# A decoder block's first norm rearranged: four lo parts on GpSimd, c spread without a diagonal, squares in pairs, 1/rms on quarters of the tokens, two more load buffers

## The chip, the core and the metric

The kernel runs on one core of one Trainium2 chip. The metric is the device time of one execution in microseconds (us), as the median of several runs. The core has a matrix engine (TensorE, PE in the rows), VectorE (DVE), ScalarE (ACT), GpSimd (POOL), and a queue from which SyncE (SP) issues loads and stores. Each engine takes its own instructions strictly in the order of the program, and waits when an operand is not there yet.

## What is computed

One decoder block for 512 tokens of width 1024: a norm whose scale and shift come from a second input c, a projection, attention and a short convolution, an output projection, a second norm, and an expert layer in which each token uses 128 of 16384 single neurons.

```python
h = modulate(rmsnorm(x, norm1_g), shift1, scale1)     # mod = silu(c) @ ada_w + ada_b, six parts of 1024
proj = h @ w_in                                       # q | k | v | conv_B | conv_C | conv_u
q, k = rope(rmsnorm(q)), rope(rmsnorm(k))             # then attention over a window of 128
conv = cb * short_conv(cc * cu, conv_w)
x = x + gate1 * (concat(rmsnorm(attn), rmsnorm(conv)) @ w_out)
x = x + gate2 * peer(modulate(rmsnorm(x, norm2_g), shift2, scale2))
```

The change touches the first line and the first products of the second.

## The kernel before

Products are kept near full precision by splitting each operand in two: `hi` is the operand rounded to the matrix engine's format, `lo` is the rest, and a product is the sum of three matmuls (hi by hi, hi by lo, lo by hi). `parts` loads a block of 128 x 1024 weights into one of five buffers (tag `ld`), ScalarE makes `hi` (L176), and VectorE subtracts and makes `lo` (L177). `hi` and `lo` have four buffers each, used in turn.

The input x lies transposed: eight tiles of 128 features x 512 tokens (`xT`). The start of the kernel goes like this:

- `rows_of` lays the 1024 numbers silu(c) out along the free axis and on all partitions (`cact`): VectorE multiplies the identity by c into eight diagonal blocks (`dg`, L156, in a load buffer), and two matmuls with a matrix of ones sum over partitions (L159).
- The sum of squares of the first norm: ScalarE squares each tile of x, VectorE adds the eight squares up in a chain (L223), one matmul with ones sums over partitions (`ss`, L253), ScalarE takes the root and VectorE the reciprocal of a 128 x 512 tile (L242), so `r1` holds 1/rms of every token on all partitions.
- Scale and shift of feature tile k come in two ways. For tiles 5, 6 and 7, matmuls against the loaded part of `ada_w` (`psr`, L272, eight per tile, two loads each) give rows from which VectorE picks the diagonal (`pick`, L290). For tiles 0 to 4, VectorE multiplies a loaded block by `cact` and sums (`junk`, L213, two per tile, one load each). Then come two small instructions (`mod` L292, `s` L293), the product of x and `r1` (`f`, L295), ScalarE's scale and shift (L296) and `hH` (L176), and VectorE's `hL` (L177).
- The tiles go in the order 5, 6, 7, 0, 1, 2, 3, 4. Among them the first four weight blocks (4, 5, 0, 1: keys, values, two of queries) are loaded and split. PE takes for each tile the three matmuls of all four blocks into `pj`: 96 matmuls of 512 columns.

Behind it, ScalarE and VectorE make sine and cosine, ScalarE reads the four results out of PSUM (`vT`, `qn`, `sq`), PE sums squares of queries and keys (`ssq`, `ss`), VectorE makes the keys' 1/rms (L242 again) and the normalized keys `qn` (L363), PE turns them (`rot`, L368), and meanwhile the next projection, P2, runs as 24 matmuls into a further `pj`. P3 and the others follow.

The code is written in one order, and a scheduler gives each engine its order from that code; pools give out buffers in turn. So a change of one instruction also moves others.

Of the kernel before, what the change touches and what calls it, by code (L numbers as in the profile page):

```python
# [7 lines left out]
F32 = mybir.dt.float32  # L8
# [5 lines left out]
AF = mybir.ActivationFunctionType  # L14
# [4 lines left out]
P = 128  # L19
T = 512  # L20
NCH = 4
D = 1024
DC = 8
# [17 lines left out]
LD = 5  # L41
# [48 lines left out]
def body(tc, p):  # L90
    nc = tc.nc
# [6 lines left out]
    cp, cp_s = pool("cp")  # L98
    dp, dp_s = pool("dp", space=bass.MemoryType.DRAM)
    psm, psm_s = pool("psm", bufs=6, space=PSUM)  # L100
    psa, psa_s = pool("psa", bufs=2, space=PSUM)
    ld, ld_s = pool("ld")
# [7 lines left out]
    def bank(name):  # L110
        return psm.tile([P, 512], F32, tag="m", name=name)
# [5 lines left out]
    xT = xp.tile([P, DC, T], F32, name="xT")  # L117
# [11 lines left out]
    ident = C("ident")  # L129
    ones = cp.tile([P, P], F32, name="ones")  # L130
    nc.vector.memset(ones, 1.0)
    eps = cp.tile([P, 1], F32, name="eps")
# [19 lines left out]

    def rows_of(dst, cols):

        dg = ld.tile([P, 8, P], F32, tag="ld", bufs=LD, name="dg")
        nc.vector.tensor_mul(dg, ident[:, None, :].to_broadcast([P, 8, P]), cols[:, :, None].to_broadcast([P, 8, P]))  # L156
        for k in range(2):
            ps = psa.tile([P, 512], F32, tag="a", name="ro")
            nc.tensor.matmul(ps, ones, dg[:, 4 * k:4 * k + 4, :], start=True, stop=True)  # L159
            nc.scalar.activation(dst[:, k * 512:(k + 1) * 512], ps, AF.Copy)  # L160

    a1, a1_s = pool("a1")
# [16 lines left out]
    def load(src):  # L179
        raw = ld.tile([P, D], F32, tag="ld", bufs=LD, name="raw")  # L180
        nc.sync.dma_start(raw, src)
        return raw
# [9 lines left out]
    def weights_of(src, by=nc.vector):  # L192

        h, l = parts(src.rearrange("p a b -> p (a b)"), by)
        return (lambda k: h[:, k * P:(k + 1) * P]), (lambda k: l[:, k * P:(k + 1) * P])
# [8 lines left out]
    def ada(cols, mark=None):  # L204

        for b in cols:
            if mark is None:
                raw = load(p["ada"][b])
            else:
                raw = a1.tile([P, D], F32, tag="ada", bufs=2, name="ada")  # L210
                after(nc.sync.dma_start(raw, p["ada"][b]), mark)
            junk = rt.tile([P, D], BF16, name="junk", **R2)
            nc.vector.scalar_tensor_tensor(junk, raw, 1.0, cact, op0=OP.mult, op1=OP.mult,  # L213
                                           accum_out=mod[:, b:b + 1])
# [4 lines left out]
    def squared(b, so_far=None):  # L219
        q = tmp("sq")  # L220
        nc.scalar.activation(q, b, AF.Square)
        if so_far is not None:
            nc.vector.tensor_add(q, q, so_far)  # L223
        return q
# [9 lines left out]
    def square(ps, b, i, n, w=None):  # L234
        q = tmp("sq")
        nc.scalar.activation(q, b, AF.Square)
        nc.tensor.matmul(ps, ones if w is None else w, q, start=(i == 0), stop=(i == n - 1))

    def rstd(ps, n):
        r = tmp("rstd")  # L240
        nc.scalar.activation(r, ps, AF.Sqrt, scale=1.0 / n, bias=eps)
        nc.vector.reciprocal(r, r)  # L242
        return r
# [3 lines left out]


    ps = bank("ss1")
    sq = None  # L250
    for k in range(DC):
        sq = squared(xT[:, k, :], sq)
    nc.tensor.matmul(ps, ones, sq, start=True, stop=True)  # L253
    r1 = rstd(ps, D)
    hH = a1.tile([P, DC, T], F32R, tag="hH", name="hH")
    hL = a1.tile([P, DC, T], F32R, tag="hL", name="hL")
    hh, hlo = (lambda k: hH[:, k, :]), (lambda k: hL[:, k, :])
# [5 lines left out]
    def ada_rows(r):  # L263

        if r % 2 == 0:
            psr[0] = psa.tile([P, 2, 2, P], F32, tag="a", name="psr")
        ps = psr[0][:, r % 2]
        for n in range(2):
            w = load(p["adaR"][r, n].rearrange("p a b -> p (a b)"))
            for i in range(4):  # L270
                kb = 4 * n + i
                nc.tensor.matmul(ps, ccol[:, kb:kb + 1].to_broadcast([P, P]), w[:, i * 256:(i + 1) * 256],  # L272
                                 start=(kb == 0), stop=(kb == DC - 1))
        return ps

    ORDER = (*range(DC - NR, DC), *range(DC - NR))
    def some_weights(m):
        for b, w in zip(FIRST, WHEN):
            if w == m:
                wj[b] = weights_of(p["w_in"][b])  # L280

    some_weights(-1)
    for m, k in enumerate(ORDER):
        if k < DC - NR:
            ada((k, 8 + k))
        else:
            ps = ada_rows(m)
            for q in range(2):
                pick = rt.tile([P, P], F32, tag="pick", name="pick", bufs=1)
                nc.vector.scalar_tensor_tensor(pick, ps[:, q, :], 1.0, ident, op0=OP.mult, op1=OP.mult,  # L290
                                               accum_out=modv[:, q, k:k + 1])
        nc.vector.tensor_add(modv[:, 0:2, k], modv[:, 0:2, k], adabv[:, 0:2, k])  # L292
        nc.vector.scalar_tensor_tensor(s1[:, k:k + 1], mod[:, 8 + k:9 + k], 1.0, S("n1g", k), op0=OP.add, op1=OP.mult)  # L293
        f = tmp("f")
        nc.vector.tensor_mul(f, xT[:, k, :], r1)  # L295
        nc.scalar.activation(f, f, AF.Identity, scale=s1[:, k:k + 1], bias=mod[:, k:k + 1])  # L296
        split(hH[:, k, :], hL[:, k, :], f)
        some_weights(m)
        if m == 4:
            nc.sync.dma_start(cs2, p["cst"][:, KEEP:])  # L300
# [831 lines left out]
```

## Time and profile before

| | us |
|---|---|
| median of three runs (1435.25 to 1436.77) | 1436.56 |
| the profiled execution | 1436.58 |
| its span on the core | 1434.8 |
| PE busy | 1385.5 |
| VectorE busy | 1229.3 |
| ScalarE busy | 616.0 |
| GpSimd busy | 442.7 |

A row of the timeline says when an instruction started, how long it took, on which engine and line, what it wrote and read, and in brackets how long its engine had been idle and whose end it waited for. The granted clock of PE is given as a share of full speed (1.00 is 2.4 GHz, 0.50 is 1.2 GHz). PE's f32 matmuls appear as two records each.

### The profile page before, as it was taken

What the parts mean: (1) busy time and instruction counts of PE and PEld (TensorE: products, weight loads), DVE (VectorE), ACT (ScalarE), POOL (GpSimd) and SP (SyncE); (2) the same over time, 40 slices, a digit from 0 to 9 for tenths busy, and PEclk for the clock granted to TensorE, in tenths of its full rate; (3) what the DMA queues carried; (4) which work ended last, traced back from release to release, by engine and by line L of the source; (5) the groups of instructions that cost most, each with busy time, mean ns of one, the idle gap of its engine ahead of it and who ended that gap; (6) DMA issues with size and microseconds to landing.
All of it is one profiled execution on the core that took longest, in us unless ns stands there. A gap on an engine that the chain in (4) does not pass through costs nothing.

```text
span 1434.8 us, 21241 instructions
## 1 busy us (share of the span) xinstructions
PE 1385.5 (97%) x7696; PEld 1218.7 (85%) x7696; DVE 1229.3 (86%) x2253; ACT 616.0 (43%) x1041; POOL 442.7 (31%) x306
## 2 busy tenths in 40 slices
PE   6999998999997999999999999999999999999998
PEld 4676776888997999999888888889999998889997
DVE  7778988789999999997668989888889979898964
ACT  4524645544634556463433333333344324333431
POOL 0000001440112320510134444456556556565400
PEclk9999999999999999999999999999999999999999
DMA  8645545322687997998999999999999999999843
GB/s 282 213 150 195 190 131 197 99 86 78 212 290 236 383 372 262 348 356 324 365 333 374 405 396 379 396 370 360 360 362 396 383 357 343 367 339 390 318 147 132
DMA packets 134376, 418.80 MB, mean 292 GB/s; under 512 B 12800, under 2 KB 39552, under 8 KB 132736
## 3 DMA queue, kind: packets, MB, share of 16 engines
q1 hardware_dynamic: 92800, 266.45, 51.6%
q0 software_dynamic: 41472, 151.01, 27.9%
q8 instruction: 60, 0.98, 0.3%
q14 instruction: 44, 0.36, 0.1%
HBM read 375.77 MB, written 41.62 MB: 291 GB/s over the span
## 4 chain that ended last, share of the span: by engine, by line
PE 62%; DVE 20%; DMA 8%; issue 7%; POOL 1%; ACT 1%; SPq 0%; DVEq 0%; POOLq 0%; ACTq 0%
PE o L997 10%; PE o L998 10%; PE o L996 10%; PE pa L200 5%; PE pa L202 5%; PE pa L201 5%; DVE lo L177 4%; DMA row<-in_vL,eG 3%; DMA ada<-in_ada 2%; PE pq L202 2%; PE pq L201 2%; PE pq L200 2%; DVE B L946 2%; DVE ga L912 2%; PE pj L200 2%
## 5 line engine op out<-in xcount | busy, mean ns | idle before, releaser
L176 ACT ACTIVATE hi<-raw 128x1024 fp32r<-128x1024 f32 x298 | 312.1, 1053 | 286.8 <-issue 91.4
L177 DVE TENSOR_TENSOR lo<-raw,hi 128x1024 fp32r<-128x1024 f32 x284 | 345.2, 1218 | 31.9 <-ACT hi L176 31.1
L202 PE MATMUL pa<-h2H,lo 128*128 128x352 f32 x1024 | 329.8, 322 | 5.6 <-DVE lo L177 5.5
L200 PE MATMUL pa<-h2H,hi 128*128 128x352 f32 x1024 | 332.3, 325 | 2.2 <-ACT sp L620 2.2
L201 PE MATMUL pa<-h2L,hi 128*128 128x352 f32 x1024 | 328.9, 321 | 0.0
L997 PE MATMUL o<-lo,wwh 128*128 128x512 f32 x768 | 299.2, 390 | 0.9 <-DVE lo L177 0.9
L996 PE MATMUL o<-hi,wwh 128*128 128x512 f32 x768 | 299.6, 390 | 0.0
L998 PE MATMUL o<-hi,wwl 128*128 128x512 f32 x768 | 298.8, 389 | 0.0
L776 POOL DMA_INDIRECT row<-in_uR,eG x128 | 186.7, 1459 | 321.3 <-PE o L998 187.8
L776 POOL DMA_INDIRECT row<-in_vL,eG x128 | 178.8, 1397 | 136.8 <-PE o L998 65.6
L784 DVE SCALAR_TENSOR_TENSOR junk<-row,h2N 128x1024 bf16<-128x1024 f32 x128 | 153.8, 1220 | 64.9 <-DMA row<-in_uR,eG 64.4
L202 PEld LDWEIGHTS pa<-h2H,lo 128*128 128x128 f32 x1024 | 192.7, 188 | 6.9 <-DVE lo L177 6.8
L200 PEld LDWEIGHTS pa<-h2H,hi 128*128 128x128 f32 x1024 | 192.2, 188 | 4.9 <-ACT sp L620 2.7
L201 PEld LDWEIGHTS pa<-h2L,hi 128*128 128x128 f32 x1024 | 192.5, 188 | 2.2
L912 DVE SCALAR_TENSOR_TENSOR ga<-row,av,ga 128x1024 f32<-128x1024 f32 x127 | 162.8, 1282 | 29.8 <-DMA row<-in_vL,eG 28.7
L998 PEld LDWEIGHTS o<-hi,wwl 128*128 128x128 f32 x768 | 144.2, 188 | 30.0
L997 PEld LDWEIGHTS o<-lo,wwh 128*128 128x128 f32 x768 | 144.2, 188 | 29.7 <-DVE lo L177 1.6
L996 PEld LDWEIGHTS o<-hi,wwh 128*128 128x128 f32 x768 | 144.2, 188 | 28.3 <-issue 0.2
L176 ACT ACTIVATE wwh<-w 128x768 fp32r<-128x768 f32 x64 | 54.1, 846 | 168.0 <-DVE w L979 120.8
L177 POOL TENSOR_TENSOR lo<-raw,hi 128x1024 fp32r<-128x1024 f32 x14 | 33.8, 2413 | 288.3 <-ACT hi L176 288.3
L978 ACT ACTIVATE w<-G 128x32 f32<-128x32 f32 x128 | 22.3, 221 | 191.3 <-DVE wwl L177 182.8
L776 POOL DMA_INDIRECT row<-in_uR,eH x32 | 43.2, 1350 | 161.7 <-DVE junk L784 74.5
(266 smaller groups left out, 1896.1 us busy)
## 6 DMA issues: line engine op xcount, KB each, us to landing
raw<-in_uL SPq DMA_DIRECT2D x128, 512.0 KB, 6.0
raw<-in_vL SPq DMA_DIRECT2D x128, 512.0 KB, 6.5
Gd<-st SPq DMA_DIRECT2D x12, 2048.0 KB, 10.2
G<-Gd SPq DMA_DIRECT2D x16, 1536.0 KB, 12.5
ada<-in_ada SPq DMA_DIRECT2D x32, 512.0 KB, 4.3
Ad<-sp SPq DMA_DIRECT2D x34, 352.0 KB, 6.5
sp<-Ad SPq DMA_DIRECT2D x34, 352.0 KB, 6.6
raw<-in_w_in SPq DMA_DIRECT2D x18, 512.0 KB, 5.2
```

The source lines that it names most:

```text
L176: nc.scalar.activation(h, f, AF.Copy)
L177: by.tensor_sub(l, f, h.bitcast(F32))
L200: nc.tensor.matmul(ps, wh(k), rh(k), start=(k == k0), stop=False)
L201: nc.tensor.matmul(ps, wh(k), rl(k), start=False, stop=False)
L202: mark[0] = nc.tensor.matmul(ps, wl(k), rh(k), start=False, stop=(k == k1))
L776: d = nc.gpsimd.indirect_dma_start(out=t, out_offset=None, in_=tab, in_offset=bass.IndirectOffsetOnAxis(ap=e, axis=0))
L784: return nc.vector.scalar_tensor_tensor(junk, t, 1.0, h, op0=OP.mult, op1=OP.mult, accum_out=a)
L912: nc.vector.scalar_tensor_tensor(ga, t, av[:, k:k + 1], ga, op0=OP.mult, op1=OP.add)
L946: nc.vector.tensor_mul(B.rearrange("p t (h a b) -> p t h a b", h=8, a=4), H[:, ts, :, None, :].to_broadcast(sh), L[:, ts, None].to_broadca ...
L996: nc.tensor.matmul(o, wh[:, cs], vh[:, hs], start=(j == 0), stop=False)
L997: nc.tensor.matmul(o, wh[:, cs], vl[:, hs], start=False, stop=False)
L998: last = nc.tensor.matmul(o, wl[:, cs], vh[:, hs], start=False, stop=(j == NJ - 1))
```

## The change

- The lo parts of the first four weight blocks are made by GpSimd, no longer by VectorE.
- `rows_of` builds no diagonal: a column of c, repeated along the free axis, is the stationary operand and the identity the moving one, eight matmuls of 128 columns in place of two of 512. It is used a second time near the end of the kernel for gate2.
- The squares are added in four pairs, no longer in a chain of eight; each pair goes to PE by itself.
- `grouped` sums a pair's squares so that the four quarters of the tokens land on four groups of 32 partitions; root and reciprocal then work on 128 x 128; `spread` brings the result back to all partitions and all tokens in PSUM by four matmuls, which stand behind the first eight `psr` matmuls on PE.
- Of the two loads of `ada` for each of tiles 0 to 4, the first now goes to the two buffers (tag `ada`) that the later loads of `ada` use; with the five `ld` buffers that makes seven.

```diff
     def rows_of(dst, cols):
-        dg = ld.tile([P, 8, P], F32, tag="ld", bufs=LD, name="dg")
-        nc.vector.tensor_mul(dg, ident[:, None, :].to_broadcast([P, 8, P]), cols[:, :, None].to_broadcast([P, 8, P]))
         for k in range(2):
             ps = psa.tile([P, 512], F32, tag="a", name="ro")
-            nc.tensor.matmul(ps, ones, dg[:, 4 * k:4 * k + 4, :], start=True, stop=True)
+            for i in range(4):
+                nc.tensor.matmul(ps[:, i * P:(i + 1) * P], cols[:, 4 * k + i:4 * k + i + 1].to_broadcast([P, P]), ident,
+                                 start=True, stop=True)
...
-            if mark is None:
+            if mark is None and b >= 8:
                 raw = load(p["ada"][b])
+            elif mark is None:
+                raw = a1.tile([P, D], F32, tag="ada", bufs=2, name="ada")
+                nc.sync.dma_start(raw, p["ada"][b])
...
+    def grouped(ps, q, first, last):
+        for c in range(NCH):
+            end = nc.tensor.matmul(ps[32 * c:32 * c + 32, 0:P], ones[:, 0:32], q[:, c * P:(c + 1) * P], start=first,
+                                   stop=last)
+        return end
+    def grouped_root(ps, n):
+        r = cp.tile([P, P], F32, tag="r", name="r", bufs=1)
+        nc.scalar.activation(r, ps[:, 0:P], AF.Sqrt, scale=1.0 / n, bias=eps)
+        nc.vector.reciprocal(r, r)
+        return r
+    def spread(r, bank=None):
+        ps = bank("rr") if bank else psa.tile([P, 512], F32, tag="a", name="rr")
+        for c in range(NCH):
+            nc.tensor.matmul(ps[:, c * P:(c + 1) * P], ident[:, 32 * c:32 * c + 1].to_broadcast([P, P]), r,
+                             start=True, stop=True)
+        return ps
...
-    sq = None
-    for k in range(DC):
-        sq = squared(xT[:, k, :], sq)
-    nc.tensor.matmul(ps, ones, sq, start=True, stop=True)
-    r1 = rstd(ps, D)
+    for k in range(0, DC, 2):
+        grouped(ps, squared(xT[:, k + 1, :], squared(xT[:, k, :])), k == 0, k == DC - 2)
+    r1 = grouped_root(ps, D)
...
-                wj[b] = weights_of(p["w_in"][b])
+                wj[b] = weights_of(p["w_in"][b], nc.gpsimd)
...
             ps = ada_rows(m)
+            if m == 0:
+                r1 = spread(r1, bank)
```

The scheduler's order changes with it. On VectorE, around the first two tiles of the norm, there stood before (a `pick` reads a `psr` row, `lo` is a weight block's rest, `s1` is the scale that ScalarE waits for):

```order
L290 SCALAR_TENSOR_TENSOR pick_173,mod_102<-psr_160,cst_83 128x128
L295 TENSOR_TENSOR f_179<-xT_85,rstd_149 128x512
L290 SCALAR_TENSOR_TENSOR pick_175,mod_102<-psr_160,cst_83 128x128
L177 TENSOR_TENSOR lo_187<-raw_184,hi_186 128x1024
L292 TENSOR_TENSOR mod_102<-mod_102,sm_81 128x2
L295 TENSOR_TENSOR f_208<-xT_85,rstd_149 128x512
L293 SCALAR_TENSOR_TENSOR s1_103<-mod_102,sm_81 128x1
```

and now:

```order
L314 SCALAR_TENSOR_TENSOR pick_194,mod_102<-psr_176,cst_83 128x128
L314 SCALAR_TENSOR_TENSOR pick_196,mod_102<-psr_176,cst_83 128x128
L316 TENSOR_TENSOR mod_102<-mod_102,sm_81 128x2
L317 SCALAR_TENSOR_TENSOR s1_103<-mod_102,sm_81 128x1
L319 TENSOR_TENSOR f_200<-xT_85,rr_189 128x512
L319 TENSOR_TENSOR f_229<-xT_85,rr_189 128x512
```

The subtraction is gone from between the picks and the scale, and `f` reads `rr`, which lies in PSUM, in place of `rstd` in SBUF.

On ScalarE, behind the last tile of the norm, there stood before (`sinT` and `cosT` are sine and cosine, `vT`, `qn` and `sq` read the four results `pj` of the first blocks, `hi_478` is the rounded block of P2):

```order
L176 ACTIVATE hH_152<-f_320 128x512
L324 ACT_TABLE_LOAD
L324 ACTIVATE sinT_428<-f_429 128x512
L327 ACTIVATE cosT_427<-f2_431 128x512
L461 ACTIVATE vT_449<-pj_326 128x512
L353 ACTIVATE qn_451<-pj_327,sm_81 128x512
L355 ACTIVATE sq_453<-pj_327 128x512
L353 ACTIVATE qn_459<-pj_328,sm_81 128x512
L355 ACTIVATE sq_461<-pj_328 128x512
L236 ACTIVATE sq_468<-pj_325 128x512
L176 ACTIVATE hi_478<-raw_476 128x1024
```

and now (`hi_499` is the rounded block of P2):

```order
L176 ACTIVATE hH_168<-f_341 128x512
L176 ACTIVATE hi_499<-raw_497 128x1024
L348 ACT_TABLE_LOAD
L348 ACTIVATE sinT_449<-f_450 128x512
L351 ACTIVATE cosT_448<-f2_452 128x512
L485 ACTIVATE vT_470<-pj_347 128x512
L377 ACTIVATE qn_472<-pj_348,sm_81 128x512
L379 ACTIVATE sq_474<-pj_348 128x512
L377 ACTIVATE qn_480<-pj_349,sm_81 128x512
L379 ACTIVATE sq_482<-pj_349 128x512
L239 ACTIVATE sq_489<-pj_346 128x512
```

The rounding of P2's block moved from behind the six that read `pj` to ahead of the table load; its buffer is that of the first of the four blocks.

On VectorE, at the keys' 1/rms, there stood before (`rstd_471` is that 1/rms, `qn_474` the normalized keys):

```order
L177 TENSOR_TENSOR lo_536<-raw_533,hi_535 128x1024
L371 TENSOR_TENSOR qn_451<-qn_451,cosT_427 128x512
L242 RECIPROCAL rstd_471<-rstd_471 128x512
L177 TENSOR_TENSOR lo_581<-raw_578,hi_580 128x1024
L363 SCALAR_TENSOR_TENSOR qn_474<-pj_325,sm_81,rstd_471 128x512
```

and now:

```order
L177 TENSOR_TENSOR lo_602<-raw_599,hi_601 128x1024
L177 TENSOR_TENSOR lo_651<-raw_648,hi_650 128x1024
L266 RECIPROCAL rstd_492<-rstd_492 128x512
L177 TENSOR_TENSOR lo_711<-raw_708,hi_710 128x1024
L387 SCALAR_TENSOR_TENSOR qn_495<-pj_346,sm_81,rstd_492 128x512
```

The subtractions of later blocks moved forward by two blocks: the one that stands between the reciprocal and the keys is now that of the fifth block behind the first four, whose `hi` takes the buffer of P2's. From ahead of the first attention scores (A0 in `PLAN`) on, the instructions of every engine stand in the same order in both kernels, but for `rows_of` near the end.

## Rows read from the trace of the kernel before

**Rows 1.** The page's first part: busy time, share of the span and instructions of each engine.

```profile
PE 1385.5 (97%) x7696; PEld 1218.7 (85%) x7696; DVE 1229.3 (86%) x2253; ACT 616.0 (43%) x1041; POOL 442.7 (31%) x306
```

**Rows 2.** Busy time in ten us behind P2 (the window, its length, then PE, PE's weight loads, VectorE, ScalarE and GpSimd with their counts, the granted clock, the share of the DMA engines, GB/s).

```profile
70.00:80.00 10.00, 10.00 (x47) 7.98 (x46) 9.04 (x14) 2.12 (x3) 0.00 (x0) 1.00 0.67 249
```

**Rows 3.** Timeline of the opening: the diagonal, the norm's sum over partitions, the first tile's `psr`, the reciprocal, the first `pick`.

```profile
5.37 1.22 DVE L156 TENSOR_TENSOR dg<-cst,ccol 128x1024 f32<-128x1024 f32 x1
...
12.89 2.07 PE L253 MATMUL ss<-sq,ones 128*128 128x512 f32 x2 [2.46 <-DVE sq L223]
...
14.76 5.44 PE L272 MATMUL psr<-raw,ccol 128*128 128x256 f32 x16
...
15.72 3.35 DVE L242 RECIPROCAL rstd<-rstd 128x512 f32<-128x512 f32 x1 [1.26 <-ACT rstd L241]
20.25 0.29 DVE L290 SCALAR_TENSOR_TENSOR pick<-psr,cst 128x128 f32<-128x128 f32 x1 [1.17 <-PE psr L272]
```

**Rows 4.** Narrow windows, columns as in rows 2: two of the `psr` matmuls, then one each of the fall and the rise of PE's level behind the four blocks, and two inside the blocks.

```profile
14.70:15.70 1.00, 1.00 (x4) 0.74 (x3) 0.00 (x0) 0.69 (x2) 0.00 (x0) 1.00 1.06 324
...
18.70:19.20 0.50, 0.50 (x4) 0.42 (x4) 0.38 (x1) 0.00 (x0) 0.00 (x0) 1.00 0.00 0
...
39.00:40.00 1.00, 1.00 (x4) 0.74 (x3) 1.00 (x3) 0.00 (x0) 0.00 (x0) 0.50 0.90 340
...
43.00:44.00 1.00, 1.00 (x6) 0.83 (x5) 1.00 (x1) 0.00 (x0) 0.00 (x0) 1.00 0.97 277
...
59.00:60.00 1.00, 1.00 (x5) 0.53 (x5) 0.28 (x1) 1.00 (x2) 0.00 (x0) 0.71 0.00 0
...
62.00:63.00 1.00, 1.00 (x3) 0.39 (x2) 0.08 (x1) 1.00 (x2) 0.00 (x0) 0.58 0.78 229
```

**Rows 5.** Timeline of PE in the later query stage: eight records of four f32 matmuls of 128 columns.

```profile
299.74 1.05 PE L738 MATMUL psc<-sk,qs 128*128 128x128 f32 x8
```

**Rows 6.** Timeline of VectorE in the norm: the two of the `lo` parts behind the first pick, a `junk` that waited for its load, the last `hL`.

```profile
21.28 1.22 DVE L177 TENSOR_TENSOR lo<-raw,hi 128x1024 fp32r<-128x1024 f32 x1
...
28.68 1.23 DVE L177 TENSOR_TENSOR lo<-raw,hi 128x1024 fp32r<-128x1024 f32 x1 [1.33 <-ACT hi L176]
...
35.57 1.23 DVE L213 SCALAR_TENSOR_TENSOR junk<-raw,cact 128x1024 bf16<-128x1024 f32 x1 [0.93 <-DMA raw<-in_ada]
...
51.56 0.68 DVE L177 TENSOR_TENSOR hL<-f,hH 128x512 fp32r<-128x512 f32 x1
```

**Rows 7.** Timeline of GpSimd around 230 us, where it makes the lo part of two blocks of the query stage.

```profile
226.89 2.60 POOL L177 TENSOR_TENSOR lo<-raw,hi 128x1024 fp32r<-128x1024 f32 x1 [226.44 <-ACT hi L176]
233.00 2.35 POOL L177 TENSOR_TENSOR lo<-raw,hi 128x1024 fp32r<-128x1024 f32 x1 [3.51 <-ACT hi L176]
```

**Rows 8.** Timeline of VectorE over the same stretch, and last the group of L293 from the view by line and shape (busy us, mean ns): the same form of instruction with smaller operands.

```profile
226.02 1.22 DVE L177 TENSOR_TENSOR lo<-raw,hi 128x1024 fp32r<-128x1024 f32 x1
227.16 2.36 DVE L554 SCALAR_TENSOR_TENSOR s<-mod,sm 128x8 f32<-128x8 f32 x1
...
232.62 0.75 DVE L544 SCALAR_TENSOR_TENSOR xT<-py,mod,xT 128x512 f32<-128x512 f32 x1
...
L293 DVE SCALAR_TENSOR_TENSOR s<-mod,sm 128x1 f32<-128x1 f32 x8 | 1.2, 153 | 0.0
```

**Rows 9.** Timeline of ScalarE behind the norm.

```profile
51.30 1.28 ACT L324 ACT_TABLE_LOAD   x1
53.34 0.64 ACT L324 ACTIVATE sinT<-f 128x512 f32<-128x512 f32 x1 [0.76 <-DVE f L323]
54.53 0.63 ACT L327 ACTIVATE cosT<-f 128x512 f32<-128x512 f32 x1 [0.56 <-DVE f L326]
55.33 0.60 ACT L461 ACTIVATE vT<-pj 128x512 f32<-128x512 f32 x1 [0.17 <-PE pj L202]
...
58.12 0.62 ACT L236 ACTIVATE sq<-pj 128x512 f32<-128x512 f32 x1
...
60.65 1.28 ACT L241 ACT_TABLE_LOAD   x1
61.94 0.69 ACT L241 ACTIVATE rstd<-ss,eps 128x512 f32<-128x512 f32 x1
...
68.13 1.06 ACT L176 ACTIVATE hi<-raw 128x1024 fp32r<-128x1024 f32 x1 [3.60 <-PE pj L201]
```

**Rows 10.** Timeline of PE at the same place: the last matmul of the four blocks, the keys' sum of squares, the transposes behind P2, the turn of the keys, the first matmul of P3. Two records of one engine may overlap.

```profile
56.26 0.39 PE L202 MATMUL pj<-hH,lo 128*128 128x512 f32 x1
...
59.22 1.88 PE L237 MATMUL ss<-sq,cs 128*128 128x512 f32 x2
...
68.16 0.60 PE L493 MATMUL vt<-cst,vT 128*128 128x128 f32 x4
69.09 1.13 PE L368 MATMUL rot<-qn,cs 128*128 128x512 f32 x2 [0.33 <-DVE qn L363]
69.65 0.79 PE L200 MATMUL pj<-hH,hi 128*128 128x512 f32 x1
```

**Rows 11.** Timeline of VectorE there: the keys' reciprocal, the lo part behind it, the normalized keys.

```profile
63.95 3.34 DVE L242 RECIPROCAL rstd<-rstd 128x512 f32<-128x512 f32 x1
67.22 1.16 DVE L177 TENSOR_TENSOR lo<-raw,hi 128x1024 fp32r<-128x1024 f32 x1
68.30 0.74 DVE L363 SCALAR_TENSOR_TENSOR qn<-pj,sm,rstd 128x512 f32<-128x512 f32 x1
```

## The prediction

> **What bounds the kernel now.** I read the page first: PE is busy for 97% of the span [rows 1], so a gain can only come from a place where PE waits or runs at its lower level, and the change touches one such place, the first 70 us. Next come the windows behind it: from 70 us on PE is busy for 10.00 of 10.00 us [rows 2], and the orders are the same again. Everything there is released by an earlier instruction or load, nothing by a date, so what the start of P3, 70.22 us (69.09 + 1.13, rows 10), gains or loses is carried to the end. I therefore work out when P3 starts after the change; the gate2 call is weighed below. The profiled execution (1436.58) stands 0.02 us from the median (1436.56), so its sums are used as they are.
>
> Three stretches lead to 70.22. In the opening the sum over partitions ends at 14.97 (12.89 + 2.07), the first tile's psr matmuls run from 14.76 to 20.20, and VectorE, its reciprocal done at 19.07, waits 1.17 us for them: the first pick is at 20.25 [rows 3]. From there to the last hL, at 51.56, VectorE is the chain; it stood still for a rounded block and for a load, 1.33 and 0.93 us [rows 6]. PE ends the four blocks at 56.65 (56.26 + 0.39), 13.57 us before P3 [rows 10].
>
> **Opening.** The reciprocal shrinks from 3.35 us to a quarter of the columns, and the diagonal and three adds go, but none of that was last: the psr matmuls were [rows 3]. They move by what happens on PE. ScalarE must still square eight tiles, so the last sum reaches PE at about 12.8, as before (12.89, rows 3); there stand four small matmuls instead of two records of 512 columns. Their price is not in the trace. The nearest row, eight records of 128 columns in 1.05 us or less [rows 5], gives 0.8 to 1.7 us over the two levels. So psr starts between 13.7 and 15.2 (at the lower pace the earlier pairs still queue on PE) instead of 14.97. Its 16 records pass at 4 a us at first and 8 a us after 18.5 [rows 4], and that change of pace weighs more than the start. PE now has matmuls almost without a gap from 5.4 on, where the diagonal used to begin [rows 3], so the faster pace may come sooner. At the earliest psr ends at 17.2, at the latest (pace as before) at 20.5. I take 18.8, near the middle, because the records say that PE is occupied but not whether matmuls of 32 columns count for its level. First pick at 19.0: **1.25 us earlier** (3.0 earlier to 0.3 later).
>
> **The norm's tiles.** Between first pick and last hL VectorE spent 31.3 us, 2.3 of it on the two waits, so 29.0 at work. Three of the four subtractions lay in it; one instruction of this size holds VectorE for 1.15 (226.02 to 227.16, rows 8), so 3.45 go and 25.6 are left. The two waits go as well: the loads start as soon as PE or GpSimd frees a buffer, and seven buffers keep the queue ahead; by the issue order each block and each ada part then lands at least 1 us before its use. If that cover fails, up to 2.3 comes back.
>
> What comes instead are waits for GpSimd. A lo part takes it 2.35 us [rows 7]. The only place where one met VectorE's arithmetic is 227 us: GpSimd's subtraction started at 226.89 while VectorE's own ran to 227.16, then VectorE's L554, on 128 x 8 numbers, took 2.36 us and ended at 229.52, just behind GpSimd's 229.49 [rows 7, 8]. The same form with smaller operands takes 0.15 [rows 8]. An instruction that reads PSUM (L544 at 232.62) ran in 0.75 beside the next one [rows 7, 8]. So I let every lo part on GpSimd hold each VectorE instruction that reads two SBUF operands: junk, hL, mod, s, but not the f, which now take r1 from PSUM, nor the picks. The Trainium skill's page "SBUF — State Buffer", section "Who interferes with whom", speaks against this change in the same sense: VectorE with two SBUF inputs contends with a GpSimd instruction that reads SBUF, and one waits for the whole of the other. By that rule each lo part could cost up to 2.35 us where VectorE used to spend 1.15 on it; the trace agrees, with one instance.
>
> Where the four fall: the first (12.5 to 15.5) and the second (about 17 to 19.5) run while VectorE waits for psr. The third comes when its block is rounded, about 25.3, and holds the second tile's s until 27.7: 1.8 us. The fourth is asked for during a junk at about 32.3, gets its turn at 33.4 and holds the fourth tile's hL from 34.1 to 35.9: 2.4 us with the wait for ScalarE ahead of it. PE's fourth block waits for the same lo part, 2.2 us, and catches up. Two turns between ScalarE and VectorE at later tiles are 0.4 us each. Together 5.0, and 0.3 for mod and s, which now follow each other directly. Last hL: 19.0 + 25.6 + 5.3 = 49.9, **1.7 us earlier** (bounds: 5 earlier with no hold and the early pace, 1.5 later with the late pace and the loads as before). Behind it PE has no backlog now, 0.7 us and eight matmuls of 0.23, and ends the blocks at 52.4 instead of 56.65.
>
> **What is late next.** Here most of that 4.2 is lost. ScalarE's order puts the rounding of P2's block ahead of the table load, sine, cosine and all reads of the four results. Its buffer is that of the first block, so it waits for that block's last matmul, 1.4 us before PE's end E. Before, ScalarE loaded the table at 51.30, had the cosine at 55.16 and began to read at 55.33, before PE had finished; it was done reading at 58.74, E + 2.1 [rows 9, 10]. Now: rounding E - 1.4 to E - 0.4, table 1.28, sine and cosine 0.6 each, to E + 2.1; then the same reads, 3.3 without their wait, to E + 5.4. ss starts 0.5 behind that as before, at E + 5.9 (59.22 was E + 2.57).
>
> From the start of ss to the end of P2 it took 8.94 us (59.22 to 68.16, rows 10), of which the granted clock was at the lower level from 59.4 to 62.8 (shares 0.71 and 0.58 of the two windows, rows 4). PE's longer idle time, 3.9 us here, will bring that level again. The same stretch without the turn of a query in it (0.87): 8.1, so P2 ends at E + 14.0. Then the second new wait: VectorE's subtraction between the reciprocal and the keys belongs to a block whose hi takes P2's buffer, so it waits for P2's end, and so do the keys, the turn and P3. Before, only ScalarE waited for that, at 68.13, with nobody behind it [rows 9], and the keys followed the reciprocal at 68.30 [rows 11]. Now: hi 0.25 + 1.0, lo 1.2, keys 0.7, turn 1.3, P3 at E + 18.5 instead of E + 13.57. The reciprocal is ready earlier, at about E + 14. So P3 starts at 52.4 + 18.5 = 70.9, and I add 0.3 for the hand-overs in the longer chain (bounds 0 to 1): 71.2, **1.0 us later**.
>
> **Edits at nothing.** gate2's call: VectorE loses one multiplication, PE has 16 records of 128 columns at 0.1 to 0.13 us [rows 5] for four of 512 at 0.4 [rows 10], 1.6 to 2.1 against 1.6; PE is the bound there, so -0.1 to +0.5, taken as 0. The two ada loads that moved behind two weight loads wait for P2's end anyway.
>
> **The rivals.**
> *GpSimd holds nobody, and the pace rises early.* For it: one instance is thin, and PE is occupied from 5.4 on. Last hL 2.5 earlier, opening 1.7 earlier: 4.2 less, but PE's 96 matmuls then limit a part of it, 0.6; P3 at 67.6, time 1434.0. Against: L554's end fits to 0.03 us.
> *The lower level lasts through all of P2* (the slower side). Its place is the 24 matmuls of P2, its price 0.2 us for each beyond those already counted, 20 of them: +4.0 us, 1441.6. It decides when the pace of P2 is still 4 a us at its end. For it: four us of idle PE and thin matmuls ahead. Against: at 59.4 the lower level was gone after 3.4 us, and low at 39 it was full again at 43 [rows 4].
> *The first pace does not rise earlier.* psr ends at 20.5: +1.6, 1439.2.
> *The table load, now on the path, holds ScalarE longer than its row.* The root at 61.94 followed its load at once (60.65 + 1.28), so I count 1.28; but behind the other load ScalarE stood 0.76 us (52.58 to 53.34, rows 9), put down to VectorE. If that is the load's own, 1438.4. The Trainium skill's page "ScalarE: Activation LUTs", section "What ACT_TABLE_LOAD costs", has a drain of about 1.38 us with each switch, which as an estimate from that page would make 1439.0; the row at 61.94 disagrees.
>
> **How the numbers follow.** The sum: 1436.58 + 1.0 = 1437.6, with its own range 1435.8 to 1439.4. What a measurement can tell from no change is about 0.2%, 2.9 us, so from 1433.7 to 1439.4. Chances: the forecast 0.52; no hold and early pace 0.13; the level through P2 0.14; late pace 0.17; the longer table load 0.04. Faster: most of the first rival with what overshoots it, 0.12. Slower: the second rival 0.14, half of the third 0.08, a rest of 0.04 from the others, 0.26. Same: 0.62. The range goes from 1434.0 to 1441.6, to both outer rivals.
>
> **What would show it.** First pick at 17.4 to 20.7. VectorE instructions of 0.15 us that take up to 2 us, ending with a GpSimd lo part, at about 27.5 and 35.9. No idle VectorE before a hi or a junk for want of a load. PE's end of the four blocks at 51 to 54, then some 4 us of idle PE while ScalarE runs sine and cosine; ss 5 to 6 us behind the end; the keys (L387) right behind a lo part that waited for P2. P3 at 69 to 73. I am wrong if VectorE's small instructions beside GpSimd take 0.15 us, if ScalarE has read the results within 2 us of PE's end, or if the shift at P3 is not the shift at the end.

## The result, and the profile after

The changed kernel takes 1450.37 us (median of 4 executions, 1448.58 to 1453.49) against 1436.66 of before beside it (1435.25 to 1438.05): ratio 1.0098, interval 1.0077 to 1.0118. That is 13.7 us slower where 1.0 was forecast, and outside the range. Repeated later (after2 below) the ratio was 1.0068 (1.0043 to 1.0093). One of the eight executions of after2 took 7387.61 us at a mean granted clock of 0.175; it is left out of all numbers. The profiled execution of after has a span of 1448.9 us, 14.1 longer than that of before.

The page: each engine's busy time, share of the span and instructions [rows 1].

```profile
PE 1397.6 (96%) x7758; PEld 1229.8 (85%) x7758; DVE 1222.8 (84%) x2244; ACT 615.6 (42%) x1041; POOL 449.9 (31%) x310
```

VectorE's timeline of after: start, duration, instruction, and in brackets the idle time ahead of it with what ended it [rows 3, 6, 8].

```profile
19.35 0.29 DVE L314 SCALAR_TENSOR_TENSOR pick<-psr,cst 128x128 f32<-128x128 f32 x1 [4.00 <-PE psr L294]
...
27.25 0.29 DVE L314 SCALAR_TENSOR_TENSOR pick<-psr,cst 128x128 f32<-128x128 f32 x1 [0.92 <-PE psr L294]
...
27.91 1.86 DVE L316 TENSOR_TENSOR mod<-mod,sm 128x2 f32<-128x2 f32 x1
...
35.46 2.27 DVE L177 TENSOR_TENSOR hL<-f,hH 128x512 fp32r<-128x512 f32 x1 [0.49 <-ACT hH L176]
...
52.31 0.69 DVE L177 TENSOR_TENSOR hL<-f,hH 128x512 fp32r<-128x512 f32 x1
...
71.38 1.23 DVE L177 TENSOR_TENSOR lo<-raw,hi 128x1024 fp32r<-128x1024 f32 x1 [2.87 <-ACT hi L176]
72.52 0.74 DVE L387 SCALAR_TENSOR_TENSOR qn<-pj,sm,rstd 128x512 f32<-128x512 f32 x1
```

GpSimd's timeline of after, the third and the fourth lo part [rows 7].

```profile
27.37 2.39 POOL L177 TENSOR_TENSOR lo<-raw,hi 128x1024 fp32r<-128x1024 f32 x1 [8.89 <-ACT hi L176]
34.13 3.04 POOL L177 TENSOR_TENSOR lo<-raw,hi 128x1024 fp32r<-128x1024 f32 x1 [4.38 <-ACT hi L176]
```

The first pick is 0.9 us earlier than before. The two long VectorE instructions end just behind a lo part on GpSimd (27.91 + 1.86 = 29.77 behind 27.37 + 2.39 = 29.76; 37.73, 0.6 behind 37.17), as forecast. Not forecast is the wait of 0.92 us for PE at 27.25: the psr matmuls of the later tiles now end last.

PE's timeline of after from the last matmul of the four blocks to P3 [rows 10]. The turn of a query at 70.27 directly follows P2's last matmul.

```profile
54.78 0.39 PE L202 MATMUL pj<-hH,lo 128*128 128x512 f32 x1
58.78 3.29 PE L381 MATMUL ssq<-cs,sq 128*128 128x2 f32 x16 [3.61 <-ACT sq L379]
61.93 2.05 PE L240 MATMUL ss<-sq,cs 128*128 128x512 f32 x2
...
70.27 1.02 PE L392 MATMUL rot<-qn,cs 128*128 128x512 f32 x2
71.12 0.60 PE L517 MATMUL vt<-cst,vT 128*128 128x128 f32 x4
73.32 1.13 PE L392 MATMUL rot<-qn,cs 128*128 128x512 f32 x2 [1.59 <-DVE qn L387]
```

The same stretch of after in windows: busy time and instructions of PE, PEld, DVE, ACT and POOL, the granted clock, the DMA share and GB/s [rows 4].

```profile
58.00:60.00 2.00, 1.22 (x7) 1.22 (x8) 0.00 (x0) 2.00 (x5) 0.00 (x0) 0.78 0.38 154
60.00:62.00 2.00, 2.00 (x11) 2.00 (x11) 0.74 (x1) 2.00 (x3) 0.00 (x0) 0.50 0.03 8
62.00:64.00 2.00, 2.00 (x4) 0.97 (x4) 2.00 (x3) 1.98 (x3) 0.00 (x0) 0.50 0.23 29
64.00:66.00 2.00, 2.00 (x6) 1.52 (x6) 1.60 (x2) 1.11 (x2) 0.00 (x0) 0.51 0.95 301
66.00:68.00 2.00, 2.00 (x11) 1.64 (x9) 2.00 (x1) 0.00 (x0) 0.00 (x0) 1.00 0.96 326
```

PE pauses for 3.61 us behind the four blocks, as forecast (3.9). Then the clock is at the lower level, 1.2 of 2.4 GHz, for about 7 us, twice as long as in before. The keys are turned at 73.32 instead of 69.09: **the head, the kernel up to P3, is 4.2 us late, not 1.0**.

The other 9.9 us of the span arise later, where the order of the work is the same. Three pauses of PE stand there in both kernels, ahead of the sum of squares over attnT (ssa), of the first matmuls on fH (pq) and of a lo part (pa). Windows of before around them, columns as above:

```profile
184.00:188.00 4.00, 3.71 (x10) 1.61 (x9) 3.42 (x6) 1.88 (x4) 0.00 (x0) 1.00 0.32 89
...
242.00:249.00 7.00, 6.94 (x30) 5.36 (x30) 6.98 (x11) 7.00 (x17) 0.00 (x0) 1.00 0.39 149
...
676.00:683.00 7.00, 7.00 (x46) 7.00 (x45) 3.49 (x5) 1.77 (x3) 0.00 (x0) 1.00 0.92 303
```

And of after:

```profile
189.00:192.00 3.00, 3.00 (x4) 1.00 (x3) 2.98 (x6) 1.67 (x3) 0.00 (x0) 0.50 0.27 46
...
248.00:253.00 5.00, 5.00 (x13) 3.79 (x12) 4.98 (x9) 5.00 (x12) 0.00 (x0) 0.50 0.49 189
...
685.00:690.00 5.00, 4.72 (x16) 4.72 (x17) 2.49 (x3) 0.58 (x2) 0.00 (x0) 0.50 0.76 247
```

The three pauses themselves, in PE's timeline of before and then of after (ssa, pq, pa):

```profile
183.50 1.98 PE L237 MATMUL ssa<-sq,ones 128*128 128x512 f32 x4 [2.80 <-ACT sq L236]
...
241.74 0.50 PE L200 MATMUL pq<-fH,hi 128*128 128x512 f32 x1 [3.04 <-ACT fH L230]
...
675.20 0.42 PE L202 MATMUL pa<-h2H,lo 128*128 128x352 f32 x1 [2.81 <-DVE lo L177]
```

```profile
188.19 5.40 PE L240 MATMUL ssa<-sq,ones 128*128 128x512 f32 x8 [2.24 <-ACT sq L239]
...
247.46 0.80 PE L200 MATMUL pq<-fH,hi 128*128 128x512 f32 x1 [3.07 <-ACT fH L233]
...
685.28 0.66 PE L202 MATMUL pa<-h2H,lo 128*128 128x352 f32 x1 [3.50 <-DVE lo L177]
```

The pause ahead of ssa is shorter in after, the one ahead of pq the same (3.04 and 3.07 us), the one ahead of pa 0.7 us longer, and only in after does the lower level follow. Going along both traces instruction by instruction, the shift grows by 1.0 us at a pause among the attention's products at 121, by 0.6 behind ssa, by 2.5 behind pq and by 2.9 behind pa, by 1.2 between 390 and 450, and by the rest among the row fetches behind 700 us.

### The profile page after: what moved, and what is told of

It reads as the page before. It is cut to its first block, busy times and chain, and to the rows that moved or that the text cites. A ratio compares the mean times of both kernels' runs of the same rounds, so it can differ in the third digit from the quotient of the medians.

```text
span 1448.9 us, 21353 instructions
## 1 busy us (share of the span) xinstructions
PE 1397.6 (96%) x7758; PEld 1229.8 (85%) x7758; DVE 1222.8 (84%) x2244; ACT 615.6 (42%) x1041; POOL 449.9 (31%) x310
## 4 chain that ended last, share of the span: by engine, by line
PE 25%; issue 11%; DVE 8%; DMA 7%; POOL 6%; ACT 0%; POOLq 0%; DVEq 0%; ACTq 0%
POOL row L800 6%; PE o L1022 5%; PE o L1021 5%; PE o L1020 5%; DMA row<-in_uR,eG 5%; PE pa L202 4%; PE pa L200 4%; PE pa L201 4%; DMA row<-in_vL,eG 3%; DVE lo L177 2%; DVE junk L808 2%; DVE ga L936 1%; DVE B L970 1%; DVE wwl L177 1%; DVE A L966 0%
## 5 line engine op out<-in xcount | busy, mean ns | idle before, releaser
L177 DVE TENSOR_TENSOR lo<-raw,hi 128x1024 fp32r<-128x1024 f32 x280 | 340.5, 1218 | 37.9 <-ACT hi L176 37.6
L177 POOL TENSOR_TENSOR lo<-raw,hi 128x1024 fp32r<-128x1024 f32 x18 | 43.8, 2431 | 286.5 <-ACT hi L176 286.5
```

The source lines that it names most:

```text
L177: by.tensor_sub(l, f, h.bitcast(F32))
```

## The experiments

Before itself ranged from 1431.1 to 1443.8 us over 140 executions on four chips (mean 1437.6), so the table gives means and says of how many. "Low time" is the time at the lower level, worked out from each execution's mean granted clock: 2 x (1 - clock) x span. The ratio is the one against before beside it on the same chip; where runs stand in one row, the interval in brackets is the widest span of theirs.

| kernel | executions | mean us | ratio to before (interval) | low time us |
|---|---|---|---|---|
| before | 140 | 1437.6 | | 28.6 |
| after (first) | 4 | 1450.7 | 1.0098 (1.0077 to 1.0118) | 36.9 |
| after2 | 7 | 1447.1 | 1.0068 (1.0043 to 1.0093) | 37.2 |
| b_d8 | 10 | 1439.9 | 1.0024 (1.0006 to 1.0043) | 30.5 |
| b_d19 | 10 | 1442.6 | 1.0028 (1.0004 to 1.0053) | 27.4 |
| a_fill | 10 | 1440.5 | 1.0022 (1.0005 to 1.0039) | 27.3 |
| b_fill | 10 | 1436.6 | 0.9989 (0.9971 to 1.0007) | 28.7 |
| u_lo | 12 | 1441.1 | 1.0020 (1.0002 to 1.0037) | 33.8 |
| u_sq | 12 | 1444.7 | 1.0046 (1.0029 to 1.0063) | 36.3 |
| u_ada | 7 | 1446.0 | 1.0062 (1.0039 to 1.0085) | 34.3 |
| u_rows | 11 | 1444.1 | 1.0050 (1.0035 to 1.0066) | 33.0 |
| b_lo | 10 | 1443.6 | 1.0044 (1.0027 to 1.0061) | 34.3 |
| a_p2fill | 12 | 1439.2 | 1.0017 (0.9998 to 1.0036) | 24.7 |
| a_p2f1 | 6 | 1445.3 | 1.0061 (1.0044 to 1.0077) | 36.1 |
| best2, best2b | 24 | 1439.2 | 1.0011, 1.0014 (0.9994 to 1.0032) | 21.9 |
| best1, best1b, best1c | 36 | 1435.1 | 0.9988, 0.9975, 0.9983 (0.9962 to 1.0006) | 22.1 |
| best4 | 12 | 1437.4 | 0.9993 (0.9977 to 1.0009) | 25.1 |

**Pure delays.** The first theory was that a delay moves the pauses, and that their new place alone brings the lower clock.

```diff
         ps = bank("pj")
+        for _ in range(8 if b == 3 else 0):      # 19 in b_d19
+            nc.tensor.matmul(ps, w[0](0), hh(0), start=True, stop=True)
         mm3(ps, w, hh, hlo)
```

> The kernel before with 8 more matmuls of 512 columns ahead of P3's own, into P3's bank (the first real one starts the sum anew), and nothing of the change: a pure delay of 8 x 0.23 = 1.8 us from 70 us on. Theory of the place: the same pauses of PE (at 181, 239 and 672 us in before) come 1.8 us later and now bring the lower clock level, so the time rises by more than the delay: 1443 us (1440 to 1448). Rival, that something in the change itself works late: a delay costs its own size and nothing else, 1438.5 us.

> The kernel before with 19 more matmuls ahead of P3's, a pure delay of 4.3 us, about the 4.2 us by which P3 is late after the change. Theory of the place: the pauses stand where they stand after the change, so the time is that of the changed kernel, 1450 us (1446 to 1453), about 9 us above the delay itself, with lower-level stretches near 124, 189, 247 and 684 us. Rival (the change itself works late): 1441.0 us, and the granted clock of before at those places.

The delays cost 2.1 and 4.8 us on average against before on the same chip, about their own 1.8 and 4.3. The theory fell in this form: one execution may gain or lose several us at a pause (b_d19 ran from 1435.1 to 1450.0), but over ten of them a shift by itself brings no more low time.

**Two later pauses filled.** PE multiplies ready operands into a bank that its next user starts anew.

```diff
+        h2[0] = h                      # the hi tile rounded last
...
     ssa = bank("ssa")
+    for _ in range(9):
+        nc.tensor.matmul(ssa, mH[:, 0, 0:P], mH[:, 0, :], start=True, stop=True)
...
+    for _ in range(12):
+        nc.tensor.matmul(early[0][1], early[0][0][0](0), h2[0][:, 0:T], start=True, stop=True)
     fs = []
```

> The changed kernel with PE kept busy in two pauses: 9 matmuls of 512 columns ahead of the sum of squares over attnT (186 us) and 12 ahead of the first ones on fH (244 us), into banks that are started anew behind them. Theory of the place: the low stretches at 189 and 247 us go, 0.6 + 2.4 us, so at most 1447.4 us; the later ones move, down to 1441. Rival (the change itself works late): 1450.4 us, since nothing else is touched.

> The kernel before with the same 21 matmuls in the same two pauses. Theory of the place: these pauses bring no low stretch in before, so nothing is to be had: 1436.7 us within 1 us. If the fillers cost time of their own (a pause that they outlast), up to 2 us more. Both theories agree here; it is the control for the fillers.

a_fill is 6.6 us below after2 (both chips' before had a mean of 1437.7 and 1437.8), with 10 us less low time, though its keys are still turned at 72.52 us, so this gain lies behind the head. b_fill is 1.2 below before, which is not told apart from none. The windows of a_fill behind the two pauses:

```profile
185.00:189.00 4.00, 3.55 (x15) 2.93 (x16) 4.00 (x7) 3.40 (x7) 0.00 (x0) 1.00 0.43 131
...
244.00:250.00 6.00, 5.34 (x23) 3.73 (x22) 5.38 (x9) 5.96 (x14) 0.00 (x0) 1.00 0.57 220
```

So the lower level behind these pauses is paid for in after and hardly in before; "the change itself works late" in some other way explains neither.

**The change again, and each part undone.** after2 is the changed kernel untouched. u_lo drops `nc.gpsimd` from `some_weights`; u_sq brings back `squared` in a chain, one matmul on `ones`, and `rstd`; u_ada sends all ada loads through `load`; u_rows brings back `dg`. The core of each, in that order:

```diff
-                wj[b] = weights_of(p["w_in"][b], nc.gpsimd)
+                wj[b] = weights_of(p["w_in"][b])
...
-    r1 = grouped_root(ps, D)
+    r1 = rstd(ps, D)
...
-            if mark is None and b >= 8:
+            if mark is None:
...
+            nc.tensor.matmul(ps, ones, dg[:, 4 * k:4 * k + 4, :], start=True, stop=True)
```

> The changed kernel again, untouched, beside many runs of before on one chip. Before itself now moves between 1431 and 1443 us from one execution to the next, so the four of after (1448.6 to 1453.5) may hold little. Theory of the place, for each execution anew (where the pauses of PE fall against the clock's steps differs between executions of one kernel): the mean is before plus the head's 4.2 us, 1442 us (1440 to 1444), with single executions from 1436 to 1450. Rival, that the change itself works late: 1450 us within 2 again.

> The changed kernel with the four lo parts back on VectorE. Theory of the hold: the two held instructions (1.7 us for mod, 1.6 for hL) take their usual 0.15 and 0.69, 3 to 4 subtractions of 1.15 come back, so the end of the four blocks and P3 stay within 1 us of the changed kernel's, and so does the time. Rival, that GpSimd's parts are what makes the head late: P3's start 3 us or more earlier than the changed kernel's, time 3 us less.

> The changed kernel with the old chain of squares, its reciprocal of 128 x 512 and no spread matmuls. By the steps of the prediction: first pick about 1.2 us later (20.3), f read from SBUF and so also held by GpSimd (up to 2 us), end of the four blocks 1 to 3 us later, time up to 3 us more. Rival, that this part of the change is what delays the third tile's matmuls on PE: the blocks end earlier than 55 us and the time falls by 1 to 3 us.

> The changed kernel with the eight loads back among the five shared buffers. By the steps of the prediction VectorE's waits for loads come back: end of the blocks 0.5 to 2.3 us later, time up to 2 us more. Rival, that five buffers were enough once the diagonal is gone and GpSimd frees its block early: no difference over 0.5 us.

> The changed kernel with the diagonal back in both places where a row is laid out. By the prediction this part costs nothing in the middle and at the end: 1447.1 within 1.5 us. Rival, that the matmuls on c keep PE and the following work in another phase: the time moves by 2 us or more either way.

after2 lies between the two expectations: 9.3 us over before. Its keys are turned at 73.38. Undoing the lo parts gives back 6.0 us of that, against my theory of the hold, which said 1 at most. The rival had said 3 us, all of it at P3; in u_lo's profile the keys are turned at 71.37, 2.0 us earlier than after2's, so the head shows a third of the gain. The squares undone give back 2.4 and the diagonal, set against before on its own chip, 2.1, each near the edge of what these runs tell (standard errors of 1.4 us); I had expected a loss and nothing. The loads give 1.1, which is inside the noise.

The part alone, on before:

```diff
-                wj[b] = weights_of(p["w_in"][b])
+                wj[b] = weights_of(p["w_in"][b], nc.gpsimd)
```

> The kernel before with the four lo parts on GpSimd and nothing else of the change. Theory that this part alone carries two thirds of the loss (putting it back gave 6.0 of 9.3 us): 1442 to 1444 us against 1437.7. Rival, that it costs only beside the other parts: 1437 to 1439.

6.7 us over before on its chip: the lo parts on GpSimd alone do most of the damage. The timelines of GpSimd and VectorE in b_lo show how they hold it; this multiply usually takes 1.22 us.

```profile
25.91 2.37 POOL L177 TENSOR_TENSOR lo<-raw,hi 128x1024 fp32r<-128x1024 f32 x1 [7.37 <-ACT hi L176]
```

```profile
26.01 3.36 DVE L213 SCALAR_TENSOR_TENSOR junk<-raw,cact 128x1024 bf16<-128x1024 f32 x1 [0.16 <-DMA raw<-in_ada]
```

**The pause behind the four blocks filled.**

```diff
-        ps = bank("pj")
+        ps = kept.pop(b, None) or bank("pj")
...
+    kept = {2: bank("pj")}                        # P2's bank, taken earlier
+    for _ in range(14):                           # 1 in a_p2f1
+        after(nc.tensor.matmul(kept[2], hH[:, 0, 0:P], hh(0), start=True, stop=True), mark[0])
     HEAD = 4
```

> The changed kernel with 14 matmuls of 512 columns (3.2 us) on PE in the pause of 3.6 us between the end of the four blocks and the squares of the queries, into P2's bank, which P2 starts anew. With them the scheduler also puts the lo part that stood ahead of the keys behind them. Theory that the head's delay is the lower clock in P2 plus that lo part: no low stretch at 58 us, keys turned at 68 us (67 to 69.5) where the changed kernel has 73.3, time 1447.1 (its mean on the same chip) less 4 to 6: 1442 (1440 to 1444). Rival, that the late reads by ScalarE themselves are the delay: keys not before 72 us, time 1446 to 1448.

> The changed kernel with 1 matmul instead of 14 in the pause behind the four blocks: VectorE's order is that of a_p2fill (the lo part behind the keys), the pause stays. Theory that the clock carries most of it: low stretch at 57 to 59 us as in the changed kernel, keys turned at 71 us (2 less than its 73.3), time before plus 7 us. Rival, that the order of the lo part carries it: before plus 2 to 3 us, as a_p2fill.

Windows of a_p2fill over the pause and P2, and PE's timeline where the keys are turned:

```profile
55.00:59.00 4.00, 3.99 (x20) 3.03 (x18) 1.23 (x2) 3.99 (x7) 0.00 (x0) 1.00 0.41 135
59.00:63.00 4.00, 4.00 (x24) 3.26 (x24) 1.82 (x2) 3.98 (x6) 0.00 (x0) 1.00 0.00 0
63.00:67.00 4.00, 4.00 (x19) 3.11 (x18) 3.41 (x2) 2.52 (x4) 0.00 (x0) 1.00 0.81 253
```

```profile
68.97 1.12 PE L392 MATMUL rot<-qn,cs 128*128 128x512 f32 x2 [1.01 <-DVE qn L387]
```

No low stretch, keys at 68.97, which is where before has them, and 8 us less than after2 (7 against each one's own before, where 4 to 6 were expected). Fourteen wasted matmuls make the changed kernel faster. a_p2f1 gave the 7 us over before that was expected, but not as expected: the scheduler put 14 of P2's own matmuls into the pause, P2 was done at 64, and the pause moved. VectorE's reciprocal, and a junk that here stands ahead of the keys, kept them back (PE's timeline, then the windows):

```profile
70.85 2.07 PE L392 MATMUL rot<-qn,cs 128*128 128x512 f32 x2 [5.36 <-DVE qn L387]
```

```profile
68.00:74.00 6.00, 3.15 (x5) 1.83 (x6) 6.00 (x9) 0.01 (x1) 0.00 (x0) 0.50 0.51 193
```

A longer pause, another low stretch, and the 7 us are back, with the lo part behind the keys all the same. Moving that part is not enough. What gains in a_p2fill isn't told apart further: PE is at work through the whole stretch there, and the scheduler has also moved the lo part behind the keys and put P2's matmuls between the sums of squares.

**All three pauses filled.** best1 is u_lo with 10, 9 and 12 fillers, best2 the whole change with 14, 9 and 12, best4 before with 3, 9 and 12; all by the two diffs above.

> The changed kernel with the lo parts on VectorE and PE kept busy in three pauses (10 matmuls behind the four blocks, 9 ahead of the sum over attnT, 12 ahead of the first on fH). Theory that the low clock stretches are what is paid for: u_lo's 1441.1 less 2 us at the blocks' end and 2 to 4 at the two later pauses: 1436 (1434 to 1438), at or below before's 1437.7. Rival, that the fillers only move the low stretches to other pauses: 1440 to 1442.

> best1 once more (the change with the lo parts on VectorE and three pauses filled), for its size: before less 1.5 us, between minus 3 and 0.

> best1 a third time (lo parts on VectorE, three pauses filled): before less 1.5 to 3.5 us, keys turned at 68 us.

> The whole change, lo parts on GpSimd included, with PE kept busy in three pauses (14, 9 and 12 matmuls). Theory that low clock stretches are what the change lost: a_p2fill's before plus 2.3 us, less 3 to 4 at the two later pauses: before less 1 (minus 3 to plus 1). Rival, that GpSimd's holds of VectorE cost in themselves: 3 us or more above best1.

> best2 once more (the whole change, three pauses filled). If GpSimd's holds of VectorE cost in themselves: again 3 to 5 us above best1c of the same chip. If the gap was chance: within 2 us of it, with keys turned at 67 to 69 us in both.

> The kernel before with 3 matmuls behind the four blocks and 9 and 12 in the two later pauses, nothing of the change. Theory of the clock: before less 1 to 3 us. If it equals best1, the other parts of the change (squares, diagonal, buffers) are worth nothing by themselves.

best1 is 2.5 us below before over 36 executions (1435.1 against 1437.6; standard errors 0.5 and 0.2), a little faster than both kernels. The gains don't add up: the two later pauses filled alone gave 6.6 us (a_fill), the first alone 7 (a_p2fill), and best2, with all three, is only 0.8 us nearer to its own before than a_p2fill. best4, nothing of the change, gains 0.9 on its chip, not told apart from none. best2 is 4.1 us above best1 in 24 against 36 executions, at the same low time, so GpSimd's lo parts, or the four more fillers that best2 has, cost something that is not the clock. It is not the head: best2 and best2b turn the keys at 67.19 and 69.52 us, best1 to best1c at 68.26, 68.09 and 68.53. Some 1.6 us of it show near 390 us. The transfers that bring the row numbers (`eH`), GpSimd's first row fetch and VectorE's first product on a row, in best2 and then in best1:

```profile
380.18 1.86 SPq L857 DMA_DIRECT2D eH<-ei  x3
```

```profile
385.82 1.88 POOL L809 DMA_INDIRECT row<-in_uR,eH  x1 [66.01 <-DVE lo L178]
```

```profile
393.14 1.23 DVE L817 SCALAR_TENSOR_TENSOR junk<-row,hN 128x1024 bf16<-128x1024 f32 x1 [5.14 <-DMA row<-in_uR,eH]
```

```profile
379.42 1.86 SPq L857 DMA_DIRECT2D eH<-ei  x3
```

```profile
383.37 1.08 POOL L809 DMA_INDIRECT row<-in_uR,eH  x1 [64.34 <-DVE eq L724]
```

```profile
389.11 1.23 DVE L817 SCALAR_TENSOR_TENSOR junk<-row,hN 128x1024 bf16<-128x1024 f32 x1 [1.83 <-DMA row<-in_uR,eH]
```

From the issue of `eH` to the fetch it took 5.64 us in best2 and 3.95 in best1. The bracket names a subtraction on VectorE, but that one runs from 384.38 to 385.60, and GpSimd's wait for the `eH` transfers ends at 384.95, in the middle of it, 0.9 us ahead of the fetch as in best1 (382.50 and 383.37). By these times the late fetch belongs to a late transfer. In best2b it is the same; the row is later, and a lo part queued behind that product keeps PE waiting 1.5 and 1.7 us that best1, best1b and best1c don't have. It doesn't come with the lo parts on GpSimd as such: in after, after2, a_fill, a_p2fill and b_lo the fetch takes 1.08 or 1.09 us and isn't late. Why the transfer is late in best2, and where the rest of the 4.1 lies, stays open.

## Why the prediction was wrong, point by point

*Read first: what P3 gains or loses is carried to the end.* **This step failed.** It counted the shift at 70 us and took PE behind it as always equally fast. In the profiled execution 9.9 of 14.1 us come later, and 7.0 of these where only after is at the lower level or is there longer (near 123, 189, 247 and 684 us, some 24 us at that level against 3.4 in before). Over many executions it is about half of the miss: the keys are turned about 5 us later (73.1 in the three profiles of after, after2 and a_fill, 68.1 in before, b_d8, b_d19 and b_fill, which are one kernel up to there), and the time is 9.3 us longer in after2. So where 1.0 was forecast for both, some 4 us were missed up to P3, and 4 us arise behind it. after2 has 9.7 us more low time than before on its chip, and as the head's own low stretches are no longer in after than in before (6.8 against 8.5 us on average in those profiles, the opening's included), the surplus lies behind the head. With PE busy such time costs nearly half of itself (the pq matmuls behind the pause start 0.43 us apart at the lower level and 0.23 at the higher), up to 4.9 us; among before's own 140 executions 1 us more of it goes with 0.28 us, which would be 2.7. That is most of what arises behind P3, or all of it. That after spends more time at the lower level is measured; that this is due to the new place of its pauses was my guess, and the pure delays speak against it. Why after meets it more often stays open.

*The opening.* The first pick came at 19.35 (19.0 forecast, 17.4 to 20.7), but not by a faster pace that begins earlier. PE's timeline and windows of after:

```profile
13.10 6.21 PE L294 MATMUL psr<-raw,ccol 128*128 128x256 f32 x16
```

```profile
17.00:18.00 1.00, 1.00 (x4) 0.73 (x4) 0.00 (x0) 0.00 (x0) 1.00 (x1) 1.00 0.90 356
18.00:19.00 1.00, 1.00 (x6) 0.90 (x5) 0.00 (x0) 0.00 (x0) 0.49 (x1) 1.00 0.59 160
```

The pace rose near 18.2, 0.2 us earlier than in before. The psr matmuls began at 13.10 instead of 14.76, ahead of the earliest start that I had allowed (13.7), and that gave the 0.9 us: the number is right in part by luck.

*The norm's tiles.* The mechanism was right and the sum too small: last hL at 52.31 instead of 49.9. The two holds came at mod and hL, the first one tile later than forecast: 1.7 us beyond the usual 0.15, and 2.1 with the wait for ScalarE ahead of it (1.8 and 2.4 forecast). Missing were PE's psr as the next bound (0.9) and 1.5 for hand-overs: neighbouring instructions of VectorE overlap by 3.6 us in total here and by 5.1 in before, where subtractions stood between small instructions that wait for each other. The end of the four blocks came at 55.17 instead of 52.4: **this term of the sum was off by 2.8**.

The Trainium skill's page "SBUF — State Buffer", section "Who interferes with whom", has a VectorE instruction with two SBUF inputs and a GpSimd instruction that reads SBUF contend, and the one that is issued later wait for the whole of the other. The traces agree at every lo part that met one (29.77 behind 29.76; in b_lo 29.37, which is 1.1 behind 28.28). The fourth lo part of after, begun 0.4 us behind a junk, was itself held: it took 3.04 us instead of 2.35.

*What is late next.* Right in its order: ScalarE read the last result at 60.28 (E + 5.1; 5.4 forecast), PE paused, the lo part stood ahead of the keys. The low level was priced as in before and lasted twice as long; with the thin ssq matmuls also at half pace, ss came 6.8 behind the end instead of 5.9. From there to P2's end it took 8.3 us (61.93 to 70.27; 8.1 forecast), and from there to P3 4.2 instead of 4.5. P3 was at 74.45 (73.32 + 1.13), 3.2 us later than forecast: 2.8 from the blocks' end and about 0.5 from here.

*The rivals.* The second, the lower level through all of P2 (+4.0 at P3), has P3 nearly where it came, but by another way: the clock rose at 66 us, 4 us before P2's end. No rival had low stretches behind 74 us. "GpSimd holds nobody" was wrong, and the table load took the row's 1.28, with sine 0.01 us behind it.

*Edits at nothing.* The diagonal was not shown to be free: undone, it gave 2.1 us back. In the one profile of u_rows the keys are turned at 71.38, 2.0 us ahead of after2's, but two profiles of one kernel differ as much (best2 and best2b), so the place isn't shown.

## What to carry to other kernels

A pause of PE can be paid for twice, as idle time and as the slower matmuls behind it; where a change moves work off one engine, look for the PE pause that it opens, and price the stretch behind it at both levels. Where single executions differ by up to 0.9 per cent, compare means of ten or more with their granted clock: four against four showed 13.7 us here, later ones 9.3. And idle matmuls in a pause are a cheap test of whether it is the pause and the clock: 14 of them took back most of the loss. Look at what else the scheduler moves with them.

## What the runs showed of the hardware

One kernel's executions differ by more than 12 us (before: 1431.1 to 1443.8), and the granted clock moves with them: the 28 executions of before with the least low time took 1434.9 us on average, the 28 with the most 1440.8. Pauses of 3.04 and 3.07 us at the same instruction left PE at 2.4 GHz in the profile of before and at 1.2 in that of after. A pause of 3.6 us behind the four blocks was followed by the lower level in every profile that had one (after, after2, a_fill, u_sq, u_ada, u_rows, b_lo); in a_p2fill, where matmuls filled it, the clock stayed at 2.4 GHz.
